# Where the expert tiles, the score products and three gathers stand in a one-core hybrid block

## The chip, the core and the metric

One core of a Trainium2 chip runs the whole kernel. Its engines work side by side, each through its own list of instructions in order: TensorE (PE, with its weight loads PEld), VectorE (DVE), ScalarE (ACT), GpSimd (POOL) and SyncE (SP, which here only issues transfers). The metric is the device time of one execution in microseconds (us); shorter is better.

## The reference

The block takes 512 tokens of width 1024. Two recurrent token mixers (RWKV-7 and mLSTM) run in parallel, are gated and merged, and their result is added to the input. Then comes the part that this study is about, a PEER layer: every token is scored against two sets of 128 keys in each of 8 heads, the best 16 pairs of keys per head pick 128 of 16384 experts, and the output is a gated sum over them:

```
s = jnp.einsum('nhpc,hpkc->nhpk', q, sub_keys.astype(F32))
s_top, i_top = lax.top_k(s, PEER_TOPK)
...
best, pos = lax.top_k(cand, PEER_TOPK)
expert = jnp.take_along_axis(cand_idx, pos, axis=-1)
gate = jax.nn.softmax(best, axis=-1)
...
act = jax.nn.gelu(jnp.einsum('tkd,td->tk', u_emb[eb], tb), approximate=False) * gb
return jnp.einsum('tk,tkd->td', act, v_emb[eb])
```

A final RMSNorm follows.

## The kernel before

**Precision.** Every large product is made in three matmuls (`mm3`, lines 92 to 95) from operands that are split into a high and a low part. `split` (lines 97 to 99) writes the high part on ScalarE (line 98, `wh`) and then the low part, a subtraction, on VectorE (line 99, `wl`). A low part is thus ready only after ScalarE and then VectorE have got to it in their lists.

**Experts.** For the last 384 of the 512 tokens no expert is gathered: all 16384 rows of `u` are multiplied, 128 experts at a time, in 128 *expert tiles*. One call of `H()` (line 871) is one expert tile: 24 matmuls into a PSUM tile `h` and a Gelu. `feed(i)` inside it issues the load of tile i + 3 and the split of tile i + 2; loaded tiles, high and low parts have three buffers each. For the first 128 tokens the experts' rows are gathered (GpSimd issues an indirect transfer of 128 x 1024 numbers per expert slot, `fly`) and multiplied by the tokens on VectorE (`land`, line 902). At most two gathers are in flight until the loop over v, then five.

**The turns** (line 1097). A loop of 21 turns, n = 0 to 20, finds the experts. Turn n makes the queries n on TensorE (`q_mm`, n < 16), splits the query weights of turn n + 2, calls `H()` once (even n up to 12) or twice (odd n; all of 13 to 15) or three times (16 to 20), makes the scores n - 1 (`s_mm`), and on VectorE finds the best keys of the scores n - 2 (`top_keys`, two blocks of tokens at a time) and goes two steps further in `pairs`, the generator that combines two key lists. `pairs` also runs sums on GpSimd (`cand`, line 1020). The calls are written out in program order, and each engine keeps that order. After the turns, 43 expert tiles are done, the last three around the transposes `tr` and ahead of `onehot(0)`.

**Expert weights.** Lines 1187 to 1210: 24 groups of 16 tokens. VectorE makes one-hot tables (`onehot`), TensorE multiplies them (`w`), the results go to DRAM as `dW`. 18 more expert tiles stand between the groups, and one `land` and `fly` in each.

**Head of the loop over v** (line 1290): six expert tiles, at the end of which the first tiles of `v`, the weights and (line 1298) `acc`, the residual rows of the first 128 tokens, are requested, and `v_split(0)` splits the first `v` tile. While it runs, three more gathers are landed and sent off. **The loop over v** (line 1315) runs j = 0 to 127: 18 matmuls `po` each, an expert tile wherever `ready` allows, and the rest of the gathers, spread by `pace`.

## Time and profile before

| | |
|---|---|
| median of three timed runs | 1859.1 us (1854.59 to 1859.84) |
| the profiled execution | 1852.99 us, of which the span is 1850.9 us |
| TensorE busy | 1785.2 us, 96% of the span |
| VectorE busy | 1379.7 us, 75% |
| ScalarE, GpSimd busy | 744.4 us (40%), 459.0 us (25%) |
| transfers | 431.40 MB, mean 233 GB/s |

All times in the rows below are from the span's start. The page's first part gives each engine's busy time; a stretch is judged by its own numbers, since the stages of this kernel have different limits. The chain that ended last runs 65% of the span through TensorE and 10% through VectorE.

### The profile page before, as it was taken

The page shows a single profiled execution, that of the slowest core. Times are in us where ns is not written, and L with a number is a line of the kernel's source. Part 1 is how long each engine was busy: PE and PEld are TensorE (multiplying, and loading weights), DVE is VectorE, ACT ScalarE, POOL GpSimd, SP SyncE. Part 2 cuts the span into 40 slices and gives each one's busy share as a digit, 9 for nine tenths or more (in the row PEclk, how much of TensorE's full clock was granted, in tenths as well). Part 3 has the DMA queues.
Part 4 walks back from the last instruction along what each step waited for, and adds up shares of the span by engine and source line. Part 5 has one row for each costly group of instructions (what it writes and reads, how often), then busy time and mean ns, then how long its engine had stood idle before and what let it go on. Part 6 is the DMA issues. An engine that isn't in the chain of part 4 may idle for free.

```text
span 1850.9 us, 27419 instructions
## 1 busy us (share of the span) xinstructions
PE 1785.2 (96%) x10281; PEld 1574.8 (85%) x10281; DVE 1379.7 (75%) x2612; ACT 744.4 (40%) x1102; POOL 459.0 (25%) x445
## 2 busy tenths in 40 slices
PE   7999989999999999899999899999999999999998
PEld 6777777887879998799999899889888989898886
DVE  6576693554665899978999467778787878887965
ACT  4575433553434333234555333333333333333433
POOL 0000001100200123210222235444444445443300
PEclk9999999999999999899999999999999999999999
DMA  4456545424725453333999988999999999898981
GB/s 180 129 162 183 163 174 173 146 80 161 238 103 179 141 167 129 117 129 120 290 288 279 330 301 310 344 326 331 330 335 316 348 320 336 314 315 310 380 277 69
DMA packets 242501, 431.40 MB, mean 233 GB/s; under 512 B 22976, under 2 KB 149568, under 8 KB 241344
## 3 DMA queue, kind: packets, MB, share of 16 engines
q1 hardware_dynamic: 143088, 257.66, 41.0%
q0 software_dynamic: 36864, 134.23, 20.6%
q10 hardware_dynamic: 62416, 37.75, 6.8%
q8 instruction: 81, 1.33, 0.3%
q14 instruction: 52, 0.43, 0.1%
HBM read 372.83 MB, written 56.75 MB: 232 GB/s over the span
## 4 chain that ended last, share of the span: by engine, by line
PE 65%; DVE 10%; DMA 2%; ACT 1%; issue 1%; SPq 1%; POOL 0%; ACTq 0%; DVEq 0%
PE po L93 9%; PE po L94 9%; PE po L95 9%; PE h L95 8%; PE h L93 8%; PE h L94 8%; PE w L1201 5%; DVE wl L99 2%; PE m L94 1%; PE m L93 1%; PE m L95 1%; DMA vf<-in_v_dram 1%; DMA wf<-in_u_t_dram 1%; PE q L93 1%; PE q L95 1%
## 5 line engine op out<-in xcount | busy, mean ns | idle before, releaser
L95 PE MATMUL h<-th,wl 128*128 128x384 f32 x1024 | 345.8, 338 | 12.1 <-DVE wl L99 12.1
L93 PE MATMUL h<-tl,wh 128*128 128x384 f32 x1024 | 347.1, 339 | 0.0
L94 PE MATMUL h<-th,wh 128*128 128x384 f32 x1024 | 344.7, 337 | 0.0
L99 DVE TENSOR_TENSOR wl<-wf,wh 128x1024 fp32r<-128x1024 f32 x208 | 251.9, 1222 | 110.7 <-ACT wh L98 110.7
L897 POOL DMA_INDIRECT gat<-in_u_dram,eid x128 | 191.4, 1495 | 382.0 <-DVE gat L902 326.2
L93 PE MATMUL po<-vl,ah 128*128 128x512 f32 x654 | 256.0, 391 | 6.6 <-DVE vl L99 6.6
L98 ACT ACTIVATE wh<-wf 128x1024 fp32r<-128x1024 f32 x208 | 217.3, 1052 | 102.1 <-PE m L94 68.0
L94 PE MATMUL po<-vh,ah 128*128 128x512 f32 x654 | 255.6, 391 | 0.0
L95 PE MATMUL po<-vh,al 128*128 128x512 f32 x654 | 255.3, 390 | 0.0
L897 POOL DMA_INDIRECT gat<-in_v_dram,eid x128 | 182.1, 1422 | 236.2 <-DVE acc L908 206.6
L99 DVE TENSOR_TENSOR vl<-vf,vh 128x1024 fp32r<-128x1024 f32 x111 | 135.8, 1224 | 134.4 <-ACT vh L98 134.4
L95 PEld LDWEIGHTS h<-th,wl 128*128 128x128 f32 x1024 | 193.7, 189 | 13.7 <-DVE wl L99 13.7
L892 ACT ACTIVATE act<-h 128x384 f32<-128x384 f32 x98 | 48.2, 492 | 382.3 <-PE h L95 382.3
L93 PEld LDWEIGHTS h<-tl,wh 128*128 128x128 f32 x1024 | 194.3, 190 | 3.1
L94 PEld LDWEIGHTS h<-th,wh 128*128 128x128 f32 x1024 | 194.0, 189 | 2.9
L908 DVE SCALAR_TENSOR_TENSOR acc<-gat,dots,acc 128x1024 f32<-128x1024 f32 x128 | 164.1, 1282 | 2.1
L93 PE MATMUL m<-hl,wh 128*128 128x512 f32 (+1 forms) x392 | 154.1, 393 | 7.3 <-DVE hl L99 5.1
L95 PE MATMUL m<-hh,wl 128*128 128x512 f32 (+1 forms) x392 | 154.8, 395 | 0.7 <-DVE wl L99 0.5
L902 DVE SCALAR_TENSOR_TENSOR gat<-gat,tok 128x1024 f32<-128x1024 f32 x128 | 152.2, 1220 | 3.5 <-DMA gat<-in_u_dram,eid 3.5
L94 PE MATMUL m<-hh,wh 128*128 128x512 f32 (+1 forms) x392 | 154.3, 394 | 0.0
L98 ACT ACTIVATE vh<-vf 128x1024 fp32r<-128x1024 f32 x111 | 117.1, 1055 | 86.5 <-issue 40.6
L93 PEld LDWEIGHTS po<-vl,ah 128*128 128x128 f32 x654 | 123.4, 189 | 31.0 <-ACT ah L98 7.6
(390 smaller groups left out, 3085.0 us busy)
## 6 DMA issues: line engine op xcount, KB each, us to landing
wf<-in_u_t_dram SPq DMA_DIRECT2D x128, 512.0 KB
vf<-in_v_dram SPq DMA_DIRECT2D x111, 512.0 KB
W<-dW SPq DMA_DIRECT2D x32, 768.0 KB
wf<-in_w_in_t_dram SPq DMA_DIRECT2D x46, 512.0 KB
dW<-stg ACTq DMA_DIRECT2D x11, 2048.0 KB
wf<-in_v_dram SPq DMA_DIRECT2D x17, 512.0 KB
wf<-in_w_q_t_dram SPq DMA_DIRECT2D x16, 512.0 KB
dA<-as SPq DMA_DIRECT2D x30, 192.0 KB
```

Of the source, the lines that this page charges most:

```text
L93: nc.tensor.matmul(ps, lh, rl, start=first, stop=False)
L94: nc.tensor.matmul(ps, lh, rh, start=False, stop=False)
L95: nc.tensor.matmul(ps, ll, rh, start=False, stop=last)
L98: nc.scalar.activation(hi, src, AF.Copy)
L99: (sub or nc.vector).tensor_tensor(lo, src, hi.bitcast(FT), op=OP.subtract)
L892: nc.scalar.activation(a, ps, AF.Gelu)
L897: nc.gpsimd.indirect_dma_start(out=t, out_offset=None, in_=src, in_offset=bass.IndirectOffsetOnAxis(ap=eid[:, j:j + 1], axis=0))
L902: nc.vector.scalar_tensor_tensor(t, t, 1.0, tok0, op0=OP.mult, op1=OP.mult, accum_out=dots[:, j:j + 1])
L908: nc.vector.scalar_tensor_tensor(acc, t, dots[:, j:j + 1], acc, op0=OP.mult, op1=OP.add)
L1201: nc.tensor.matmul(ps[:, r], og[k][:, a, :, r], O1[:, a, :, r], start=k == 0, stop=k == 1)
```

## The change

- `q_half` (the first two query tiles, made in two halves of the tokens) multiplies the high part of the tokens through first, and the low part afterwards.
- In the turns the second `H()` is called after `q_lo`, the first half of `top_keys` and `fly`, and the third after the second half of `top_keys`. `s_mm` follows the second tile where there are two or more. From turn 13 on, the low part that the second call splits is made on GpSimd.
- The two expert tiles that stood ahead of `onehot(0)` stand behind it.
- The head of the loop over v lands no gathers and sends none off until it is over, and `acc` is loaded at j = 8 of the loop.

```diff
@@ q_half
-            mm3(ps[:, cs], h[:, k], l[:, k], th[:, k, cs], tl[:, k, cs], c == 0 and k == 0, c == 1 and k == KD - 1)
+            nc.tensor.matmul(ps[:, cs], h[:, k], th[:, k, cs], start=c == 0 and k == 0, stop=False)
+            nc.tensor.matmul(ps[:, cs], l[:, k], th[:, k, cs], start=False, stop=False)
+        for k in range(KD):
+            nc.tensor.matmul(ps[:, cs], h[:, k], tl[:, k, cs], start=False, stop=c == 1 and k == KD - 1)
@@ the turns
-        for _ in range(3 if n > 15 else 2 if n > 12 else 1 + n % 2):
-            H()
-        if 1 <= n <= 16:
+        tiles = 3 if n > 15 else 2 if n > 12 else 1 + n % 2
+        H()
+        if 1 <= n <= 16 and tiles == 1:
             s_mm(n - 1)
         t = n - 2
         step()
...
         if 0 <= t < 16:
             top_keys(t, (0, 1))
         fly()
+        if tiles > 1:
+            U.sub = nc.gpsimd if n > 12 else nc.vector
+            H()
+            U.sub = nc.vector
+            if 1 <= n <= 16:
+                s_mm(n - 1)
         step()
         if 0 <= t < 16:
             top_keys(t, (2, 3))
             if t % 2:
                 live.append(pairs(t // 2))
+        if tiles > 2:
+            H()
         if n < 13:
             land(1)
@@ after the turns
-    H()
-    H()
...
     onehot(0)
+    H()
+    H()
@@ head of the loop over v
-            nc.sync.dma_start(acc, x1[0:128, :])
         if hn == AHEAD + SPILL - 1:
             v_split(0)
-        if hn < AHEAD + SPILL - 2:
-            land(1)
-            fly()
...
     for j in range(NK):
+        if j == 8:
+            nc.sync.dma_start(acc, x1[0:128, :])
```

Three places in the order of the instructions. The first is VectorE at the end of turn 17 and the start of turn 18 (`itop` are the last of the best keys of turn 17, `wl` the low parts of expert tiles, `i`, `dl` and `best` the first work of `pairs` in turn 18). Before:

```order
L1009 MAX_INDEX itop<-stop,mr_0_7967 128x8
L1009 MAX_INDEX itop<-stop,mr_1_7968 128x8
L99 TENSOR_TENSOR wl<-wf,wh 128x1024 x3
L1025 CAST i_8088<-itop 128x64
L1026 TENSOR_TENSOR dl<-i_8088 128x4x15
L1029 TENSOR_TENSOR dl_8091<-dl,dst_5131 128x256
L1001 MAX best<-cand 128x8 x4
```

And in the change:

```order
L1012 MAX_INDEX itop<-stop,mr_0_7934 128x8
L1012 MAX_INDEX itop<-stop,mr_1_7935 128x8
L99 TENSOR_TENSOR wl<-wf,wh 128x1024 x2
L1028 CAST i_8022<-itop 128x64
L1029 TENSOR_TENSOR dl<-i_8022 128x4x15
L1032 TENSOR_TENSOR dl_8025<-dl,dst_5131 128x256
L1004 MAX best<-cand 128x8 x4
```

Before, the three low parts belong to turn 18 (tiles 33 to 35). In the change the two are tile 32, the last of turn 17, and tile 33, the first of turn 18.

The second place is GpSimd from the sums of turn 18 to the table `iota`, which the one-hot stage needs. Before:

```order
L1020 TENSOR_TENSOR cand<-stop 128x4x3
L1020 TENSOR_TENSOR cand<-stop 128x4x2 x3
L1022 TENSOR_TENSOR cand<-stop 128x4x8
L1032 CAST i_8093<-itop 128x256
L1165 CAST iota_8483<-iota 128x512
```

And in the change:

```order
L1023 TENSOR_TENSOR cand<-stop 128x4x3
L1023 TENSOR_TENSOR cand<-stop 128x4x2 x3
L1025 TENSOR_TENSOR cand<-stop 128x4x8
L1035 CAST i_8027<-itop 128x256
L99 TENSOR_TENSOR wl<-wf,wh 128x1024 x3
L1174 CAST iota_8417<-iota 128x512
```

Three of the eight low parts that GpSimd takes over (those of turns 18, 19 and 20) now stand between the sums and the table; the low part of an even turn always follows that turn's sums.

The third place is VectorE ahead of the one-hot stage (`gB` and `g` are the gates, `O` and `Og` the tables of the first group of tokens). Before:

```order
L1152 TENSOR_TENSOR gB<-gf,gA 128x384
L1153 COPY g_4788<-best 128x128
L99 TENSOR_TENSOR wl<-wf,wh 128x1024 x2
L1177 TENSOR_TENSOR O_8485<-iota_8483,i2T 128x2048
L1180 TENSOR_TENSOR Og_8488<-O_8485,gB 128x2048
L1180 TENSOR_TENSOR Og_8487<-O_8485,gA 128x2048
L1182 TENSOR_TENSOR O_8491<-iota_8483,i1T 128x2048
```

And in the change:

```order
L1163 TENSOR_TENSOR gB<-gf,gA 128x384
L1164 COPY g_4788<-best 128x128
L1186 TENSOR_TENSOR O_8419<-iota_8417,i2T 128x2048
L1189 TENSOR_TENSOR Og_8422<-O_8419,gB 128x2048
L1189 TENSOR_TENSOR Og_8421<-O_8419,gA 128x2048
L1191 TENSOR_TENSOR O_8425<-iota_8417,i1T 128x2048
L99 TENSOR_TENSOR wl<-wf,wh 128x1024 x2
```

The two low parts have moved from ahead of the four tables to behind them.

## Rows read from the trace of the kernel before

**Rows 1.** TensorE's waits in the whole span: total us, times, longest us.
```profile
PE h L95 <- DVE wl L99: 12.1, 3, 5.6
PE po L93 <- DVE vl L99: 6.6, 3, 4.7
PE w L1201 <- DVE O L1182: 3.3, 1, 3.3
PE q L93 <- DVE tl L99: 2.0, 2, 1.7
```

**Rows 2.** Windows by stage: length, busy by engine (instructions), granted clock, DMA share, GB/s.
```profile
620.00:845.00 225.00, 211.62 (x1154) 198.99 (x1153) 206.11 (x860) 71.61 (x106) 49.81 (x80) 0.97 0.42 138
...
1028.00:1060.00 32.00, 27.32 (x151) 26.66 (x150) 13.42 (x17) 11.78 (x17) 6.36 (x6) 0.95 0.93 324
1060.00:1300.00 240.00, 240.00 (x1185) 215.84 (x1185) 184.89 (x274) 81.93 (x115) 111.81 (x74) 0.99 0.92 323
...
1677.00:1720.00 43.00, 41.11 (x181) 33.41 (x180) 36.83 (x44) 15.24 (x21) 13.96 (x12) 1.00 0.97 337
```

**Rows 3.** Timeline of TensorE, tiles 27, 33, 34 and 35: start, us, line.
```profile
783.36 0.69 PE L95 MATMUL h<-th,wl 128*128 128x384 f32 x1 [5.60 <-DVE wl L99]
...
814.60 0.69 PE L95 MATMUL h<-th,wl 128*128 128x384 f32 x1 [2.90 <-DVE wl L99]
...
820.02 0.33 PE L93 MATMUL h<-tl,wh 128*128 128x384 f32 x1
...
824.18 0.33 PE L93 MATMUL h<-tl,wh 128*128 128x384 f32 x1
```

**Rows 4.** Windows behind two of these waits: columns as in rows 2.
```profile
814.60:816.00 1.40, 1.40 (x4) 1.40 (x5) 1.40 (x2) 0.00 (x0) 1.40 (x1) 0.50 0.47 73
...
1057.89:1064.76 6.87, 6.87 (x19) 5.46 (x20) 6.31 (x9) 3.02 (x5) 1.68 (x1) 0.58 0.85 276
```

**Rows 5.** Timeline of VectorE, low parts in turns 5, 13, 17 and 18.
```profile
621.67 1.23 DVE L99 TENSOR_TENSOR wl<-wf,wh 128x1024 fp32r<-128x1024 f32 x1 [0.90 <-ACT wh L98]
...
740.23 3.49 DVE L99 TENSOR_TENSOR wl<-wf,wh 128x1024 fp32r<-128x1024 f32 x3
...
794.34 1.21 DVE L99 TENSOR_TENSOR wl<-wf,wh 128x1024 fp32r<-128x1024 f32 x1
796.26 1.23 DVE L99 TENSOR_TENSOR wl<-wf,wh 128x1024 fp32r<-128x1024 f32 x1 [0.72 <-ACT wh L98]
800.66 1.23 DVE L99 TENSOR_TENSOR wl<-wf,wh 128x1024 fp32r<-128x1024 f32 x1 [3.17 <-ACT wh L98]
...
813.33 3.48 DVE L99 TENSOR_TENSOR wl<-wf,wh 128x1024 fp32r<-128x1024 f32 x3
```

**Rows 6.** Timeline of GpSimd, two-input work of four kinds.
```profile
498.55 1.30 POOL L745 TENSOR_TENSOR pg<-pg,mf 128x512 f32<-128x512 f32 x1 [4.38 <-DVE pg L701]
...
528.47 2.40 POOL L847 TENSOR_TENSOR tok<-tok,xs 128x1024 f32<-128x1024 f32 x1 [15.59 <-DVE xs L827]
...
601.36 1.58 POOL L1020 TENSOR_TENSOR cand<-stop 128x64 f32<-128x64 f32 x8 [45.50 <-DVE stop L1007]
...
781.80 5.21 POOL L1020 TENSOR_TENSOR cand<-stop 128x64 f32<-128x64 f32 x8 [21.49 <-DVE stop L1007]
```

**Rows 7.** Timeline of VectorE beside the first of them.
```profile
498.60 1.80 DVE L99 TENSOR_TENSOR wol<-wo,woh 128x512 fp32r<-128x512 f32 x1 [0.19 <-ACT woh L98]
```

**Rows 8.** Timeline of VectorE ahead of the one-hot stage.
```profile
852.17 1.22 DVE L99 TENSOR_TENSOR wl<-wf,wh 128x1024 fp32r<-128x1024 f32 x1
...
857.14 1.22 DVE L1177 TENSOR_TENSOR O<-iota,i2T 128x2048 f16<-128x2048 f16 x1
```

**Rows 9.** Timelines in the head: SyncE's queue, GpSimd's third gather there, ScalarE.
```profile
1041.73 0.38 SPq L1298 DMA_DIRECT2D acc<-x  x1
...
1044.32 1.68 POOL L897 DMA_INDIRECT gat<-in_u_dram,eid  x1 [6.82 <-DVE gat L902]
...
1053.83 1.06 ACT L98 ACTIVATE wh<-wf 128x1024 fp32r<-128x1024 f32 x1 [8.41 <-DMA wf<-in_u_t_dram]
```

## The prediction

> **What bounds the kernel now.** TensorE does, and where it stands still it stands for VectorE. I read its waits over the whole span first [rows 1]: 12.1 us in three waits of expert tiles for a low part, 6.6 us of the products with v (one of 4.7 us, two short ones near the end), 3.3 us for the first one-hot table, 2.0 us for the tokens' low part. The change touches each of these four lines, so I priced them one by one. The stages [rows 2] say whose limit each is. In the turns VectorE is busy 206.11 of 225 us and TensorE 211.62, so both are near the bound. In the head, 1028 to 1060, neither is, but transfers take 0.93 of what they can. In the loop over v TensorE is busy 240.00 of 240.00 us: what is saved ahead of it stays saved, and what is put into it costs nothing unless transfers (0.92) or VectorE become the limit.

> [...]

> **The turns.** The last wait there is what counts: tile 33 at 814.60, behind the first low part of turn 18, which VectorE begins at 813.33 [rows 3, 5]. Behind it TensorE waits for no low part of this stage any more. So I ask how much earlier VectorE ends turn 17, and how far TensorE has come by then.

> VectorE ends turn 17 earlier by these pieces. Five low parts (turns 13 to 17, one each) go to GpSimd, at 3.49/3 = 1.16 us each [rows 5], 5.8 us. The third low part of turn 17 is moved behind the turn's key work, another 1.2. In turn 17 VectorE waits 0.72 and 3.17 us for ScalarE's high part, while the key work behind it could run; in the new order that work comes first, 3.9. A like wait of 0.90 in turn 5 [rows 5], the last one before VectorE is busy without a break, goes too. Sum 11.8 us: about 801.5 instead of 813.3.

> TensorE gives part of it back. Before, tile 34 starts 820.02 - 813.33 = 6.7 us after that point. In the new order the first low part there is tile 32's, so 1.2 us later tile 32 starts, then 33, and tile 34 at 1.2 + 2 x 4.16 = 9.5. That is 2.8 us lost and 9.0 won.

> GpSimd and VectorE hinder each other. A GpSimd addition ran from 498.55 to 499.85; the VectorE subtraction that began 0.05 us after it took until 500.40, 1.80 us [rows 6, 7], ending 0.55 us after GpSimd did. The other way round, GpSimd's eight sums took 1.58 us at 601.36 and 5.21 at 781.80, beside 3.4 us of low parts [rows 6]. No row shows a low part on GpSimd; the nearest is a product of the same size, 2.40 us [rows 6]. In even turns it follows the sums and meets VectorE's searches for maxima, which read one input. In the odd turns 13, 15 and 17 it is free to start in VectorE's two-input work, and I charge half its length, 1.2 us, each: 3.6. The ends are nothing (9.0 remain) and all five at full length, 12.0 (a loss of 3.0). I take 9.0 - 3.6 = 5.4 us.

> [...]

> The rest of the move costs nothing. The scores are 12 matmuls that TensorE makes in any case, and in turn 16 they now come ahead of the tile that waited 5.60 us at 783.36 [rows 3]. Each moved tile takes its load with it in SyncE's list, but the load of tile i + 3 was held by the low part of tile i before as well. In eight places that load and ScalarE's next high part now wait for GpSimd; behind them on ScalarE stands the Gelu that frees the tile's PSUM buffer, and with two buffers a tile of 4.16 us is in hand. If that cover fails, the loss is the last rival's.

> **One-hot stage.** The first table is begun at 857.14, behind a low part at 852.17 and another [rows 8]. With both behind the tables it can begin at about 852.2, 5 us earlier, more than the wait of 3.3 us [rows 1]. The two low parts are not needed until the next expert tile, a whole group of products later. I take 3.3; the lower end is 0, if GpSimd, which now has three low parts ahead of the table of numbers (3 x 2.40 us, spread over three turns), is late with it.

> **The head.** v's first low part stands on ScalarE behind the high part of expert tile 67, which waits 8.41 us for a transfer until 1053.83 [rows 9]; TensorE then starts at 1057.89 [rows 4], 4.06 us behind it, having waited 4.7. So that load must land 4.7 us earlier for the wait to go. Ahead of it the change removes `acc` (issued at 1041.73) and three gathers (the last at 1044.32 [rows 9]), each 128 x 1024 x 4 bytes = 0.52 MB. At 324 GB/s [rows 2] each is 1.6 us. `acc` alone is the lower end, 1.6; all four are 6.5. The three gathers that follow in the same place wait no longer for VectorE and may come sooner, so I count `acc` and two gathers, 4.9 us: the wait is gone, and with it the slow clock. 4.7 + 2.9 = 7.6; for a remainder I take 7.0. The four transfers and three gather products (3 x 1.2 us on VectorE) go into the loop over v, where 8% of some 620 us of transfer time is free and 6.5 us are needed. Without that cover, near the loop's end (share 0.97 [rows 2]), they would cost up to those 6.5.

> **First queries.** At most the 2.0 us of rows 1, at least 0. Both high and low parts of the last tokens come in two pieces, and the last low piece must be followed by its products in either order; nearer the lower end: 0.3.

> **Sum.** 5.4 + 3.3 + 7.0 + 0.3 = 16.0 us. The profiled execution took 1853.0 us (span 1850.9 and 2.1 around it), so it would take 1837.0. The median of the timed runs, 1859.1, is 6.1 above the profiled one, and I forecast on its scale: 1843 us.

> **Rivals.**
> 1. *Every wait of the turns goes*, because GpSimd's share frees VectorE entirely: 12.1 idle and 1.6 of slow clock at each of three waits, 16.9, with 3.3, 7.6 and 0.3: 28 us, 1831. Against it: the first of the three waits, in turn 14, is for a low part of turn 13's start, ahead of everything that goes to GpSimd, and only 0.90 of it can go. Chance 0.10.
> 2. *The head keeps its wait*, since the remaining gathers rush into the gap: 1.6 there, 10.6 in all, 1848.5. For it speaks that VectorE no longer holds them back. Chance 0.15.
> 3. *Each low part holds VectorE up for its whole length*: the turns lose 3.0, in all 7.6 us are won, 1851.5. For it speaks the row at 498.60; against it, that in even turns VectorE is then at one-input work. [...] Chance 0.13.
> 4. *Slower: GpSimd's low part becomes what TensorE waits for.* If it is stretched as the sums were, 5.21/1.58 = 3.3 times, it takes 7.9 us. In turn 18 it can end 1.58 + 2.3 + 2.4 = 6.3 us after VectorE's first low part begins (the sums, two low parts of 1.16 that hold them up, itself), or some 7.5 with the small work between, and is wanted at 9.5: 2 us of slack. So eight tiles would each be 5.5 - 2 = 3.5 us late, 28 us, against 16 won: 1871. It decides at 2.7 us late each, a low part of 7.1 us on GpSimd. Against it: the sums' excess of 3.6 is the 3.4 us of two-input work beside them, not a factor. Chance 0.07.

> **How the numbers follow.** My case has 0.55, with its own range of 1839 to 1850 (turns 1.8 to 9.0 by three odd low parts at 0 to 2.4 us, head 4 to 7.6). Two runs of this kernel can be told apart from about 0.3%, 5.6 us. Faster than that: my case, rivals 1 and 2 and half of 3: 0.87. Within it: the rest of 3 and a mild 4: 0.07. Slower: 0.06. Rivals 1 and 4 lie outside 1832 to 1853, which holds the rest, somewhat over 0.8.

> **What the profile after should show.** Eight low parts on GpSimd of 2.4 to 4 us, and no more than some 7 us of waits of `h` for low parts, at tiles 21, 27 and 32. A first one-hot product without a wait. In the head no wait of `po` above 1 us and no stretch of low clock. In the loop over v TensorE still without a gap. Wrong would make me: low parts on GpSimd above 5 us, VectorE rows of 2 us and more beside them, or tile 67's load still landing under 2 us earlier relative to the last one-hot product.

## The result and the profile after

The changed kernel takes 1844.4 us (median of six runs, 1839.6 to 1846.0), the kernel before 1857.9 beside it (six runs, 1854.6 to 1859.8): 13.5 us less, with 16.1 forecast. The ratio of the runs' means is 0.9924, 95% interval 0.9909 to 0.9939. The profiled execution took 1846.01 us, its span is 1844.2.

The view of waits, TensorE's lines that answer to [rows 1] (total us, times, longest us; `q` was split over two lines of code, and `th` is the tokens' high part):

```profile
PE h L95 <- DVE wl L99: 10.2, 4, 3.6
...
PE q L820 <- ACT th L98: 1.8, 2, 1.0
PE po L93 <- DVE vl L99: 1.4, 2, 1.1
```

The line of `w` and `O` is gone, `po` has lost its 4.7 us, but `h` still waits 10.2 us where it waited 12.1. These are its four waits, of expert tiles 20, 21, 27 and 32:

```profile
733.84 0.45 PE L95 MATMUL h<-th,wl 128*128 128x384 f32 x1 [0.69 <-DVE wl L99]
748.81 0.69 PE L95 MATMUL h<-th,wl 128*128 128x384 f32 x1 [3.56 <-DVE wl L99]
...
789.11 0.69 PE L95 MATMUL h<-th,wl 128*128 128x384 f32 x1 [2.85 <-DVE wl L99]
814.89 0.45 PE L95 MATMUL h<-th,wl 128*128 128x384 f32 x1 [3.11 <-DVE wl L99]
```

The windows that answer to [rows 2], moved to the same work (columns as there):

```profile
627.00:851.00 224.00, 213.79 (x1165) 201.26 (x1164) 206.29 (x857) 75.59 (x111) 64.46 (x88) 0.97 0.43 139
...
1029.00:1061.00 32.00, 31.69 (x178) 30.65 (x177) 14.18 (x16) 13.14 (x19) 3.28 (x3) 1.00 0.90 300
1061.00:1301.00 240.00, 240.00 (x1195) 216.22 (x1194) 187.67 (x280) 83.11 (x116) 114.39 (x77) 1.00 0.94 330
1671.00:1714.00 43.00, 41.84 (x184) 34.02 (x183) 37.43 (x45) 15.41 (x21) 14.19 (x12) 1.00 0.97 342
```

In the head TensorE is busy 31.69 of 32 us (27.32 before) at a granted clock of 1.00. In the turns VectorE is as busy as before, 206.29 us, although GpSimd took low parts over: that is the first sign that something there was given back.

Where did the time go? The starts of the stages on TensorE's timeline, of the kernel before (first queries, first expert tile, transposes, first one-hot product, first tile of the head, first products with v, the tile behind them):

```profile
543.54 0.36 PE L93 MATMUL q<-tl,wh 128*128 128x256 f32 x1
558.85 0.34 PE L93 MATMUL h<-tl,wh 128*128 128x384 f32 x1
844.98 0.82 PE L1145 MATMUL tr<-ident,sel 128*128 128x128 f32 x6
861.94 2.28 PE L1201 MATMUL w<-O,Og 128*128 128x128 f16 x18 [3.29 <-DVE O L1182]
1027.97 0.42 PE L93 MATMUL h<-tl,wh 128*128 128x384 f32 x1
1057.89 0.77 PE L93 MATMUL po<-vl,ah 128*128 128x512 f32 x1 [4.68 <-DVE vl L99]
1064.76 0.34 PE L93 MATMUL h<-tl,wh 128*128 128x384 f32 x1
```

And the same seven marks of the changed kernel:

```profile
550.77 0.36 PE L820 MATMUL q<-th,wh 128*128 128x256 f32 x1
565.82 0.34 PE L93 MATMUL h<-tl,wh 128*128 128x384 f32 x1
849.55 0.82 PE L1156 MATMUL tr<-ident,sel 128*128 128x128 f32 x6
863.05 1.23 PE L1212 MATMUL w<-O,Og 128*128 128x128 f16 x9
1029.08 0.42 PE L93 MATMUL h<-tl,wh 128*128 128x384 f32 x1
1054.62 0.47 PE L93 MATMUL po<-vl,ah 128*128 128x512 f32 x1 [0.31 <-DVE vl L99]
1058.82 0.34 PE L93 MATMUL h<-tl,wh 128*128 128x384 f32 x1
```

The changed kernel is 7.2 us *late* at the first queries, ahead of everything that was changed. That is the spread between executions: in the eleven other profiled executions of this study this mark lies between 541.35 and 551.31, with the same code up to it. So only differences of marks are compared:

| stage | before | after | won | forecast |
|---|---|---|---|---|
| first queries | 15.31 | 15.05 | 0.3 | 0.3 |
| turns (first tile to transposes) | 286.13 | 283.73 | 2.4 | 5.4 |
| to the first one-hot product | 16.96 | 13.50 | 3.5 | 3.3 |
| groups | 166.03 | 166.03 | 0.0 | 0 |
| head (two marks, to 1064.76 and 1058.82) | 36.79 | 29.74 | 7.05 | 7.0 |
| from there to the end of the span | 786.1 | 785.4 | 0.7 | 0 |

Together 13.9 us, close to the 13.5 of the medians. Three terms came out within 0.2 us; the turns gave under half of theirs. Each entry comes from one execution of either kernel. In the eleven executions of this study with the changed order of the first queries, that stage took 15.0 us eight times and 16.6 three times, these three at a granted clock of 0.90 instead of 1.00, so its 0.3 us is not clear of the spread.

Eight low parts stand on GpSimd, 2.38 to 2.68 us each. Five of them (start, us):

```profile
748.45 2.54 POOL L99 TENSOR_TENSOR wl<-wf,wh 128x1024 fp32r<-128x1024 f32 x1
766.35 2.40 POOL L99 TENSOR_TENSOR wl<-wf,wh 128x1024 fp32r<-128x1024 f32 x1
772.32 2.40 POOL L99 TENSOR_TENSOR wl<-wf,wh 128x1024 fp32r<-128x1024 f32 x1 [3.56 <-ACT wh L98]
...
800.25 2.68 POOL L99 TENSOR_TENSOR wl<-wf,wh 128x1024 fp32r<-128x1024 f32 x1 [6.78 <-ACT wh L98]
...
830.47 2.39 POOL L99 TENSOR_TENSOR wl<-wf,wh 128x1024 fp32r<-128x1024 f32 x1 [10.64 <-ACT wh L98]
```

And VectorE's rows beside those of the odd turns 13, 15, 17 and 19, with the first low parts of turn 18 at 813.62:

```profile
748.67 2.86 DVE L1047 TENSOR_TENSOR ge<-pf,st 128x1024 f16<-128x1024 f16 x1
751.57 0.69 DVE L1050 TENSOR_TENSOR ge<-ge,dl 128x1024 f16<-128x1024 f16 x1
...
773.77 2.03 DVE L99 TENSOR_TENSOR wl<-wf,wh 128x1024 fp32r<-128x1024 f32 x1
...
800.00 0.69 DVE L1047 TENSOR_TENSOR ge<-pf,st 128x1024 f16<-128x1024 f16 x1
800.72 2.77 DVE L1050 TENSOR_TENSOR ge<-ge,dl 128x1024 f16<-128x1024 f16 x1
...
813.62 2.38 DVE L99 TENSOR_TENSOR wl<-wf,wh 128x1024 fp32r<-128x1024 f32 x2
...
830.59 2.32 DVE L1062 TENSOR_SCALAR vi<-vi 128x64 int32<-128x64 int32 x1
```

Each of these lengthened rows begins while GpSimd makes a low part and ends after it, by no more than its own usual length: 748.67 + 2.86 = 751.5, where GpSimd ends at 748.45 + 2.54 = 751.0; 773.77 + 2.03 = 775.8 and 774.7; 800.72 + 2.77 = 803.5 and 802.9. `ge` takes 0.69 us otherwise, a low part 1.22, so the low parts of turns 13, 15 and 17 cost VectorE 2.17 + 0.81 + 2.08 = 5.1 us. Beside the low part at 766.35 (turn 14) stand searches for maxima, and none is longer than elsewhere: two `MAX8` on 128x128 take 0.48 us at 767.23, as they do at 755.25, where GpSimd is idle.

### The profile page after: what moved, and what is told of

Read it like the earlier page. It is cut to its first block, busy times and chain, and to the rows that moved or that the text cites. A ratio compares the mean times of both kernels' runs of the same rounds, so it can differ in the third digit from the quotient of the medians.

```text
span 1844.2 us, 27415 instructions
## 1 busy us (share of the span) xinstructions
PE 1787.8 (97%) x10281; PEld 1575.9 (85%) x10281; DVE 1376.9 (75%) x2604; ACT 744.0 (40%) x1102; POOL 478.8 (26%) x453
## 4 chain that ended last, share of the span: by engine, by line
PE 68%; DVE 7%; DMA 3%; ACT 1%; issue 1%; SPq 0%; POOL 0%; DVEq 0%; ACTq 0%
PE po L93 9%; PE po L94 9%; PE po L95 9%; PE h L95 8%; PE h L93 8%; PE h L94 8%; PE w L1212 5%; DMA dW<-stg 1%; PE q L93 1%; PE q L94 1%; PE q L95 1%; PE m L94 1%; PE m L95 1%; DVE wl L99 1%; PE m L93 1%
## 5 line engine op out<-in xcount | busy, mean ns | idle before, releaser
L95 PE MATMUL h<-th,wl 128*128 128x384 f32 x1024 | 346.5, 338 | 10.2 <-DVE wl L99 10.2
L99 DVE TENSOR_TENSOR wl<-wf,wh 128x1024 fp32r<-128x1024 f32 x200 | 243.5, 1225 | 105.1 <-ACT wh L98 104.9
L900 POOL DMA_INDIRECT gat<-in_v_dram,eid x128 | 186.3, 1455 | 231.7 <-DVE acc L911 209.1
L95 PEld LDWEIGHTS h<-th,wl 128*128 128x128 f32 x1024 | 194.1, 190 | 12.1 <-DVE wl L99 12.1
L95 PEld LDWEIGHTS po<-vh,al 128*128 128x128 f32 x654 | 122.8, 188 | 25.8
```

Source lines behind the costliest of these rows:

```text
L95: nc.tensor.matmul(ps, ll, rh, start=False, stop=last)
L99: (sub or nc.vector).tensor_tensor(lo, src, hi.bitcast(FT), op=OP.subtract)
L900: nc.gpsimd.indirect_dma_start(out=t, out_offset=None, in_=src, in_offset=bass.IndirectOffsetOnAxis(ap=eid[:, j:j + 1], axis=0))
```

## The experiments

**Theory.** In the odd turns of the change a GpSimd low part takes 1.16 us off VectorE and costs it 0.8 to 2.2 (the rows above), depending on which instruction happens to begin beside it. The turns' gain is the order and the even turns. **Rivals:** the low parts on GpSimd are the gain; or they cost the same wherever they stand. For the head: each transfer that left it counts for itself; rival: one kind of them alone was in the way.

All runs against the kernel before on the same chip. "Turns" and "head" are the stages of the table above, from the same marks; the one-hot stage was 13.50 or 13.51 and the groups 166.02 or 166.03 in every run. The two columns come from one profiled execution of each run:

| run | turns | head | median us | ratio to before, interval |
|---|---|---|---|---|
| the change | 283.73 | 29.74 | 1844.4 | 0.9924 (0.9909 to 0.9939) |
| after_again | 283.00 | 29.47 | 1843.3 | 0.9924 (0.9912 to 0.9936) |
| old_turns | 286.29 | 29.78 | 1846.4 | 0.9947 (0.9927 to 0.9967) |
| gp_none | 284.39 | 31.00 | 1844.6 | 0.9933 (0.9920 to 0.9945) |
| gp_even | 280.37 | 29.60 | 1842.8 | 0.9931 (0.9918 to 0.9943) |
| gp_late | 277.89 | 29.43 | 1837.2 | 0.9905 (0.9892 to 0.9919) |
| gp_late5 | 274.49 | 29.47 | 1836.8 | 0.9889 (0.9874 to 0.9904) |
| gp_late_no13 | 275.42 | 30.18 | 1835.9 | 0.9886 (0.9867 to 0.9904) |
| gp_both | 270.81 | 30.71 | 1833.2 | 0.9875 (0.9861 to 0.9890) |
| acc_back | 280.18 | 30.54 | 1842.0 | 0.9920 (0.9902 to 0.9939) |
| land_back | 281.13 | 33.24 | 1846.3 | 0.9940 (0.9920 to 0.9960) |

Equal code spreads in these columns: the four runs whose turns are those of the change (the change, after_again, acc_back, land_back) lie between 280.18 and 283.73, and the nine whose head is that of the change (all but acc_back and land_back) between 29.43 and 31.00. The medians were taken on more than one chip, so they are compared by their ratios to the kernel before, or between runs of one chip.

### The turns as before: old_turns

```diff
-        tiles = 3 if n > 15 else 2 if n > 12 else 1 + n % 2
-        H()
-        if 1 <= n <= 16 and tiles == 1:
+        for _ in range(3 if n > 15 else 2 if n > 12 else 1 + n % 2):
+            H()
+        if 1 <= n <= 16:
             s_mm(n - 1)
...
-        if tiles > 1:
-            U.sub = nc.gpsimd if n > 12 else nc.vector
-            H()
...
-        if tiles > 2:
-            H()
```

> The changed kernel with the turns written as before: tiles together at a turn's start, no low part on GpSimd. Theory (the turns are worth 2.4 us, the rest of the change is worth the same without them): the stretch from the first expert tile to the first transpose is 286 us, one-hot stage and head stay at 13.5 and about 29.7, the time 1847. Rival A (the turns' part has a hidden cost or gain later): the other stages move by over 1 us. Rival B (the order alone costs time and GpSimd hid that): the stretch is below 283.

The turns are 286.29 (286.13 before), the other stages stand within their spread: the parts of the change add up, and neither rival holds.

### No low part on GpSimd, or only in even turns: gp_none, gp_even

```diff
-            U.sub = nc.gpsimd if n > 12 else nc.vector
+            U.sub = nc.gpsimd if n > 12 and n % 2 == 0 else nc.vector
```

This is gp_even; gp_none has no such line, so that every low part is VectorE's.

> All low parts stay on VectorE; the rest is the changed kernel. Theory (in odd turns a low part on GpSimd holds VectorE up by about what it takes off it): VectorE gets 5 x 1.16 = 5.8 us back before the last wait of the turns and is rid of 5.1 us of lengthened rows; the stretch from the first expert tile to the first transpose, 283.7 us in the change and 286.1 before, is 284.4, the time about 1845. Rival (the low parts on GpSimd are what the turns won): the stretch grows by 5.8 to 289.5, the time to 1850.

> Low parts on GpSimd in the even turns 14 to 20 alone; those of turns 13, 15, 17 and 19 go back to VectorE. Theory: 3 x 1.16 = 3.5 us come back to VectorE before the last wait, 5.1 us of lengthened rows go (2.2, 0.8 and 2.1 in turns 13, 15 and 17): the stretch is 1.6 shorter, 282.1, the time about 1843. Rival (each low part that GpSimd makes is worth its length): the stretch is 3.5 longer, 287.2, the time 1848.

Counted from the first expert tile, VectorE begins the first low part of turn 18 at 247.8 us in the change, 248.5 without GpSimd and 246.1 with the even turns alone: 0.7 later and 1.7 earlier, as the theory has it to 0.1 us. So all five low parts together were worth 0.7 us to VectorE in that execution, and the two of even turns alone more than all of them. In the other three executions of the change's turns VectorE gets there at 247.1, 245.9 and 246.8 us, 246.9 on average over the four: by that all five are worth 1.6 us, and the three of the odd turns cost 0.8. The medians lie too close together to show it, and gp_even's stage lies inside the spread of the change. The order by itself won 1.7 to 1.9 us (gp_none against 286.13 and 286.29, one execution each). gp_even's stage is 1.7 us shorter than expected, because the clock did not fall after its last wait (1.00 was granted behind it, 0.69 in the change; below).

### Low parts beside the searches: gp_late, gp_late5, gp_late_no13, gp_both

```diff
+            if n > 12 and n % 2:
+                nc.gpsimd.tensor_copy(mark, qs[n][1][:, 0:1].bitcast(FT) if n < 16 else behind[0])
             U.sub = nc.gpsimd if n > 12 else nc.vector
             H()
```

The copy of one number makes GpSimd wait for VectorE's last two-input work ahead of the searches (`ql`, or in turn 17 and later `qr`, kept in `behind`). In these turns `fly` stands behind the tile. gp_late5 does so from turn 5 on (`n > 4`), gp_late_no13 is gp_late5 without turn 13, and gp_both also calls the first `H()` of the even turns from 6 on behind `step` and `q_lo`, with GpSimd for its low part.

> As the change, but in the odd turns from 13 on GpSimd's low part waits for the last two-input operation ahead of VectorE's searches for maxima, so that it runs beside the searches. Theory (what counts is which VectorE instruction stands beside it): the lengthened rows go, VectorE reaches turn 18 5.1 us earlier, the stretch is 278.7, or up to 1.7 less if a slow clock goes with a wait; the time 1838 to 1840. Rival (a low part on GpSimd costs VectorE the same wherever it stands, or TensorE waits for the delayed ones): 283.7 or more, 1844 or more.

> As gp_late, and the second low part of turns 5, 7, 9 and 11 goes to GpSimd in the same way, with the gather of those turns behind it. Theory (VectorE's work bounds the turns from turn 5 on): 4 x 1.16 = 4.6 us more off VectorE, the stretch about 274, the time 1833 to 1836. Rival (the waits that are left hang on the start of turns 13 and 14 alone, or on ScalarE's high parts): no more than 1 us better than gp_late.

> The delayed low parts on GpSimd in turns 5, 7, 9, 11 and 14 to 20; that of turn 13, for which TensorE waited 2.6 us at 750 in the run with all of them, is VectorE's again. Theory: that wait and its slow clock go (2.6 + 1.3), VectorE takes 1.2 more: the stretch is 272 (274.5 with it on GpSimd), the time about 1834. Rival (VectorE is the bound up to turn 18, the wait for GpSimd lies inside it): 275.5, 1838.

> As the run with delayed low parts from turn 5 on, and in the even turns from 6 on GpSimd also makes the first low part, behind the sums and VectorE's split of the queries. Theory (VectorE's two-input work in the turns is what TensorE waits for): 6 x 1.16 = 7.0 us more off VectorE up to turn 16, the 6.6 us of waits that were left go, the stretch is 268 to 271 (274.5 without), the time 1830 to 1833. Rival (GpSimd, with sums and two low parts of 2.4 us in a turn of 11 to 13 us, is what TensorE waits for next): waits for low parts of GpSimd, the stretch 274.5 or more.

In gp_late the low parts of turns 13, 15 and 17 cost VectorE 0.7 us together, where those of the change cost 3.3 to 5.1. VectorE's timeline in turn 15 and, last, in turn 19, and GpSimd's beside turn 15:

```profile
775.68 0.47 DVE L1010 MAX8 stop<-mr 128x8 f32<-128x128 f32 x2
...
776.60 0.96 DVE L1047 TENSOR_TENSOR ge<-qr,iq 128x1024 f16<-128x1024 f16 x1
...
823.23 2.85 DVE L1050 TENSOR_TENSOR ge<-ge,i 128x1024 f16<-128x1024 f16 x1
```

```profile
774.61 2.40 POOL L99 TENSOR_TENSOR wl<-wf,wh 128x1024 fp32r<-128x1024 f32 x1
```

The search takes 0.47 us for its two, 0.48 elsewhere; only `ge`, which begins 0.4 us before GpSimd is through, takes 0.96 for 0.68. In turn 19, which has no search to stand beside, a `ge` is still held for 2.2 us, but behind TensorE's last wait. The turns are 277.9, 5.8 us less than in the change's own profile and 2.3 less than in the shortest of the four executions of its turns, and the rival (the same cost wherever it stands) falls; on the same chip the median is 5.6 us under gp_even's and 7.4 under gp_none's. With turns 5 to 11 it is 274.5, as expected, though the median moved by only 0.4 us and missed its 1833 to 1836; in the profiled execution the first queries took 16.55 us, at a granted clock of 0.90, for 15.04 in gp_late, where their code is the same.

gp_late_no13 was a miss: 275.4, as its rival said. The wait of 2.6 us for GpSimd lay inside VectorE's own lateness; one of 3.4 us for VectorE took its place. gp_both takes VectorE's lateness itself away. Its view of waits for the turns shows what is left:

```profile
PE h L95 <- POOL wl L99: 2.4, 2, 2.0
```

TensorE waits for no low part of VectorE any more, and 2.4 us for GpSimd, which is thus next in line. It is the fastest version, 10.1 us under the change's median on the same chip (after_again).

### The change once more: after_again

> The changed kernel itself once more. Theory (what the turns win hangs on where GpSimd's odd low parts fall among VectorE's instructions, and on whether the last wait is long enough to be followed by the slow clock): the stretch is between 280.2 and 283.7, as in the three executions of these turns so far, and differs from 283.7 by the lengthened rows and by 1.6 us of clock. Rival (each execution of one program takes the same there): 283.7.

283.00. With acc_back and land_back, whose turns are the same code, there are four executions: 283.73, 283.00, 281.13, 280.18, so 2.4 to 6.0 us won against 286.13, 4.1 on average. Two things make the difference. The first is where GpSimd's low part falls, which ScalarE's high part sets: in turns 15 and 17 GpSimd stood idle for 3.56 and 6.78 us until it came in the change, for 2.48 and 8.05 in acc_back. In acc_back that of turn 15 ran beside the searches and that of turn 17 beside a short operation (VectorE's rows there):

```profile
768.60 1.21 DVE L99 TENSOR_TENSOR wl<-wf,wh 128x1024 fp32r<-128x1024 f32 x1
...
796.71 1.30 DVE L1059 TENSOR_TENSOR vi<-v,i 128x64 int32<-128x64 f32 x1
```

1.21 for 2.03, and 1.30 for 0.23; that of turn 13 held the same `ge` in all four. So 3.3 us were lost in all, with 5.1 in the profile of the change (4.3 and 4.4 in the other two). The second is the clock. The windows behind the last wait, of the change (3.11 us of waiting, 22 matmuls) and of acc_back (1.14 us):

```profile
814.89:820.43 5.54, 5.54 (x22) 5.54 (x23) 5.14 (x37) 0.00 (x0) 4.93 (x9) 0.69 0.61 194
```

```profile
807.89:812.10 4.21, 4.21 (x24) 4.21 (x25) 3.84 (x25) 0.08 (x1) 4.21 (x9) 1.00 0.71 212
```

In acc_back tile 33 begins at 811.82, so the same 22 matmuls took 3.93 us: 1.6 less. With the 1.95 us by which VectorE came to turn 18 earlier, that makes the 3.55 between the two stages.

### The head: acc_back, land_back

```diff
@@ acc_back: head, and not at j == 8
             v_load(1)
+            nc.sync.dma_start(acc, x1[0:128, :])
@@ land_back: head
             v_split(0)
+        if hn < AHEAD + SPILL - 2:
+            land(1)
+            fly()
```

> The changed kernel with the load of acc put back into the head. Theory (the wait of the head is for transfers, and each of the four that left it is worth its own 0.52 MB): tile 67's high part comes 1.1 to 1.6 us later, the head (last one-hot product to the second expert tile behind it that stands after the first products with v; 29.7 us in the change, 36.8 before) is 31 to 34, the upper end if the slow clock comes back with the wait; the time 1846 to 1848. Rival (the gathers alone were in the way): 29.7, 1844.

> The changed kernel with the landings and gathers put back into the head, acc still at j = 8. Theory (transfers): three of the four transfers are back, tile 67's high part comes 2.8 to 3.3 us later than in the change, the wait and the slow clock return, the head is 33 to 36 us, the time 1848 to 1850. Rival (acc alone was in the way, standing in SyncE's list ahead of the loads): 29.7 to 30, 1844.

The high part of tile 67 in the change and in land_back (ScalarE's timeline):

```profile
1050.55 1.06 ACT L98 ACTIVATE wh<-wf 128x1024 fp32r<-128x1024 f32 x1 [4.04 <-DMA wf<-in_u_t_dram]
```

```profile
1051.89 1.06 ACT L98 ACTIVATE wh<-wf 128x1024 fp32r<-128x1024 f32 x1 [5.91 <-DMA wf<-in_u_t_dram]
```

From the head's first tile this is 21.5 us in the change, 22.3 in acc_back, 23.4 in land_back (its head begins at 1028.54) and 25.9 before. In the nine executions whose head is that of the change it lies between 21.2 and 22.5. land_back lies outside, so the gathers count (1.9 us against the change, 2.8 to 3.3 expected), and its rival, `acc` alone, falls. acc_back, with 0.8 us for 1.1 to 1.6 expected and a head of 30.5 for 31 to 34, lies inside: that `acc` alone counts is not shown, and its rival, the gathers alone, is not excluded. Both together are worth 4.4 us, more than the two one by one; why is open. The clock adds to it: behind `po`'s waits of 0.3, 1.1, 2.2 and 4.7 us the stretch to the next tile takes 4.20, 4.18, 5.81 and 6.87 us, at a granted clock of 1.00, 1.00, 0.71 and 0.58 [rows 4].

## Why the prediction was right

Measured were 1844.4 us for 1843 forecast. That the two lie 1.4 us apart is in part luck: 2.6 us less were won than forecast, and the kernel before, measured again, was 1.2 us faster than the 1859.1 that the forecast started from. By the prediction's steps:

- **One-hot stage and head: right in mechanism and size** (3.5 and 7.05 us). No run put the old order ahead of the one-hot stage back by itself; for it speak the wait of 3.3 us that is gone and the 13.5 us of every later run. The 0.3 us of the first queries came out as forecast, inside the spread of that stage. In the head tile 67 came 4.4 us earlier, for 4.9 counted, and the stretch behind `po`'s wait took 4.20 us at a clock of 1.00 for 6.87 at 0.58, so the slow clock gave back 2.7, for 2.9 (0.42 of the 6.87 us [rows 4]). That `acc` and two gathers at 1.6 us each make up the 4.9 was not borne out one by one: the size was right, its division is not settled.
- **The loop over v** took the four transfers and three products at no cost: TensorE is busy 240.00 of 240.00 us in the window read, and the rest of the span is 0.7 us shorter in the profile. In the runs of the table it lies between 785.4 and 788.6 us (786.1 before), so a cost of a few us in some executions is not excluded.
- **The turns: right in mechanism, one size off.** VectorE came to turn 18's low parts 254.5 us after the first tile before and 247.8 after, 6.7 earlier; with the 5.1 us of lengthened rows that is 11.8, the sum of the pieces; in the other three executions the two add up to 11.7, 11.9 and 12.1. The step that was off is "I charge half its length, 1.2 us, each: 3.6": the rows cost 5.1 there, 3.3 to 4.4 in the other three executions. They were not half-lengthened: in turns 13, 15 and 17 of that profile the two-input instruction that began beside GpSimd's ended 0.5, 1.1 and 0.6 us after it, and in turns 15 and 17 which one that was changed between the executions. The second size is "2.8 us lost" by TensorE, in tiles of 824.18 - 820.02 = 4.16 us [rows 3]: 4.3 in this profile and 2.7 in acc_back, since I left out the slow clock behind a last wait that was still there (0.69 over 5.54 us). The turns won 2.4 us in this profile and 4.1 on average over the four executions, for 5.4 counted.
- **Rivals.** 1 fell (10.2 us of waits stayed). Its 1.6 us of slow clock are 0.30 of the 5.42 us from 814.60 to 820.02, at a granted clock of 0.70; behind the other two waits of before it was 0.72 from 742.64 to 748.64 and 0.68 from 783.36 to 789.36, 1.7 and 1.9 us. 2 fell: the three gathers did rush, but to 1026.84 to 1030.72, about the head's start at 1029.08 and not into its gap:

```profile
1026.84 0.94 POOL L900 DMA_INDIRECT gat<-in_u_dram,eid  x1 [0.30 <-PE w L1212]
1029.48 0.94 POOL L900 DMA_INDIRECT gat<-in_u_dram,eid  x1 [1.70 <-PE w L1212]
1030.72 0.93 POOL L900 DMA_INDIRECT gat<-in_u_dram,eid  x1 [0.30 <-issue]
```

- Rival 3 was half true: in turns 13 and 17 an instruction was held for most of the low part (2.2 and 2.1 us of 2.5 and 2.7), in turn 15 for 0.8, in the even turns none. That the searches of the even turns would go free was an assumption of mine, which none of the rows of before shows. They did: two took their usual 0.48 us beside the low part of turn 14, and 0.47 in gp_late beside the one at 774.61, where a `ge` took 0.96 for 0.68. Rival 4 fell: no GpSimd low part took over 2.7 us.
- **Of the signs announced**, VectorE rows of 2 us and more came (four of them), and the waits of `h` stayed at 10.2 us instead of 7. The rows belong to the term that was off. Of the waits, those of tiles 20 and 21, 4.3 us, end no later than 0.4 us after GpSimd's first low part begins, and gp_none, with none on GpSimd, has 4.3 us there too; only the 2.9 at tile 27 and the 3.1 at tile 32 can come from the lengthened rows.

## What to carry over

In this kernel a low part moved from VectorE to GpSimd was priced by the VectorE instruction that began beside it, not by its own length alone (1.16 us): those of turns 13, 15 and 17 cost VectorE 3.3 to 5.1 us together where they fell by themselves, 0.7 where a dependency put them beside searches (gp_late). Put it there with a dependency, since an unpinned one can land beside another instruction in each execution, as in turns 15 and 17. In a program whose early part spreads by 10 us between executions, compare stage marks, and look at how long each wait was before counting what it costs, because the clock behind it can add to that: it cost 1.6 us behind one of 3.11 us in the change and 2.7 behind one of 4.68 before, and stood at 1.00 behind one of 2.01 in gp_even.

## What was unexpected in the hardware

```profile
809.31:813.30 3.99, 3.99 (x23) 3.99 (x24) 3.12 (x17) 0.00 (x0) 3.99 (x10) 1.00 0.70 200
```

```profile
814.33:818.30 3.97, 3.97 (x15) 3.97 (x16) 3.10 (x7) 0.00 (x0) 3.97 (x9) 0.62 0.66 201
```

In the stretch ahead of it gp_none had waited 1.07, 0.76 and 2.31 us, gp_even 0.76 and 1.01; what decides between the two was not tried.
